# RWKV-7 units of a two-layer recurrent trunk: the centring of the values moved behind the second products, and one cast moved from VectorE to ScalarE

## The chip, the cores and the metric

The kernel runs on one core of one Trainium2 chip. The metric is device time in microseconds, from the start to the end of one execution. The kernel before took 2766.95 us (median of 3 runs, 2766.32 to 2776.49).

The engines are named as in the profile: PE is TensorE's matrix product and PEld its weight load, DVE is VectorE, ACT is ScalarE, POOL is GpSimd, SP is SyncE, which here only issues DMAs. ScalarE and GpSimd issue DMAs as well.

## The reference, cut to what matters

The model has two layers over 1024 positions of width 1024. Layer 0 is not touched by the change. Layer 1 is RWKV-7 time mixing with 32 heads of 64 channels:

```python
r, k_raw, v = x_r @ w_r, x_k @ w_k, x_v @ w_v
...
def step(state, inp):
    r_t, w_t, k_t, v_t, kk_t, a_t = inp
    s_kk = jnp.einsum("bhvk,bhk->bhv", state, kk_t)
    state = (state * w_t[:, :, None, :]
             - s_kk[..., None] * (kk_t * a_t)[:, :, None, :]
             + v_t[..., None] * k_t[:, :, None, :])
    y_t = jnp.einsum("bhvk,bhk->bhv", state, r_t)
    return state, y_t
...
mean = jnp.mean(y, axis=-1, keepdims=True)
y = ((y - mean) * lax.rsqrt(var + GN_EPS)).reshape(bsz, s, RW_WIDTH) * lnx_g + lnx_b
```

The kernel takes the scan in chunks of 64 positions. Inside a chunk the recurrence becomes a triangular system, whose inverse is worked out and then multiplied in. Because the output is centred over the 64 channels of a head anyway, the kernel centres the values `v` before the recurrence (a product with `cent`, the identity less 1/64).

## The kernel before, in words

Layer 1 is cut into 32 **units**: a quarter of the positions (256, `qt`) by a pair of 128-channel blocks (`pp`), so eight 64-by-64 chunks for each of the two heads in a block. Each unit goes through stages, written as generators that stop at every `yield`:

- `stage_g` (L935): the three projections `g<-x,w_kr`, `g<-x,w_r`, `g<-x,w_v`, 96 steps of six matmuls; their weights come by DMAs that SyncE issues.
- `stage_a` (L968): decays, normalised keys and the products `pa` of a chunk; its L1007 to L1014 (a clamp, Ln, Exp and products) stand around the change, and L987, L983 and L991 are early work of a later unit.
- `stage_i` (L1065): the inversion of the 32-by-32 triangles, step by step on VectorE (L1084, L1086), with a DMA round trip before (L1039, L1070) and after it (L1089, L1093).
- `stage_v` (L1097): `pvt`, the values centred and turned (8 matmuls), which ScalarE copies in four pieces into the two `uv` tiles (L1106); at its second step `pr`, a product with `uv`, copied to `ar` (L1114).
- `stage_l` (L1118): the two halves of the inverse joined (`pl`, behind VectorE's transpose L1124).
- `stage_s` (L1155): first the product of the inverse `xb` with `ar`, in two halves (`p1` in the code, `p<-ar,xb` in the profile). Each half is read from PSUM three times: `t1`, called T1 here (L1168, ScalarE), and the two halves of the partitions of `uv` (L1169 on VectorE, L1170 on ScalarE). Then `p2` (`p<-am,t` in the profile), which reads `t1` and `am`, again in two parts, read by VectorE as `gm` and `rp` (L1183, L1184); then `ph` and `py`, and the state's steps over four chunks (`sts`, `sper`, L1221).
- `stage_n` (L1229): the norm of the output.

**The order.** `program` (L1351) is a list written by hand, run once for each of the units `s`: `s0` takes the next step of `stage_s` for unit `s`, `i1`, `v1` and `l1` a step of those stages for unit `s + 1`, `a2` a step of `stage_a` for unit `s + 2`, and a number that many steps of `stage_g` for unit `s + 3`. TensorE's instructions all go through `mm` and `tr` (L881, L884), which pin them to exactly this order. The other engines' instructions are put in order by the framework's planner, with a timeline of its own; it may take work of a later unit forward where it sees an engine free.

**Shared space.** The PSUM tile of `p1`, `p2` and `pvr` is one bank with one buffer (`s` in L859 to L867): the second half of `p1` can only start when all three readers of the first half have ended, and `p2` only when all three of the second have. `pvt`, `pr0` and `pl` share another (`b`). `uv` has four buffers, two for each unit. In units 4 and 5 of each quarter (and near them) `stage_x` (L809) mixes the inputs of the next quarter, on ScalarE (L829, L832), VectorE (L830) and GpSimd (L833).

Of the kernel before, what the change touches and what calls it, by code (L numbers as in the profile page):

```python
# [31 lines left out]
def trunk_kernel(ctx: ExitStack, tc: tile.TileContext, I, out, dbg=None):  # L32
    nc = tc.nc
    V, S, G, PE = nc.vector, nc.scalar, nc.gpsimd, nc.tensor
# [566 lines left out]
    ur = (slice(64, 128), slice(0, 64))  # L601
# [195 lines left out]
    for p in range(NPAIR):  # L797
        for _ in range(-(-len(left) // (NPAIR - p))):
            j, q = left.pop(0)
# [49 lines left out]
    def W1(tag, bufs=1, shape=(P, TH), dtype=F32, name=None):  # L849
        return w1p.tile(list(shape), dtype, tag=tag, bufs=bufs, name=name or tag)  # L850
# [18 lines left out]
    def pu(use):  # L869
        return pp[0].tile([P, 512], F32, tag=pmap[use], bufs=pcnt[pmap[use]], name=use)  # L870
# [10 lines left out]
    def mm(*args, **kw):  # L881
        return pin(PE.matmul(*args, **kw))  # L882
# [177 lines left out]
    def cs(c):  # L1060
        return slice(c * 64, c * 64 + 64)
# [93 lines left out]
    def stage_s(u):  # L1155


        qt, pp_ = u["qt"], u["pp"]
        lc, pt, am, ar, uv = (u[n_] for n_ in ("lc", "pt", "am", "ar", "uv"))


        t1 = W1("t1", bufs=1, shape=(P, 8, 64))
        for q in range(2):
            p1 = pu("p1")
            for j in range(4):
                mm(p1[:, j * P:(j + 1) * P], xb[:, q * 4 + j, :], ar[:, :, q * 4 + j, :], start=True, stop=True)
            p1 = p1.rearrange("p (j s c) -> p j s c", s=2, c=64)
            S.copy(t1[:, q * 4:q * 4 + 4], p1[:, :, 0])  # L1168
            V.tensor_copy(uv[q][ur[0], 0], p1[ur[0], :, 1])  # L1169
            S.copy(uv[q][ur[1], 1], p1[ur[1], :, 1])  # L1170
            yield

        gm = W1("gm", bufs=1, shape=(P, NCH, 64))
        rp = W1("rp", bufs=1, shape=(P, NCH, 64))
        for e in range(2):
            p2 = pu("p2")
            for g in range(4):
                for h in range(2):
                    mm(p2[hr[h], g * P:(g + 1) * P], t1[ur[e], 2 * g + h, :],
                       am[g // 2][ur[e], h, 2 * (g % 2) + e, 64:192], start=True, stop=True,  # L1180
                       tile_position=(ur[e].start, hr[h].start))
            p2 = p2.rearrange("p (g s c) -> p g s c", s=2, c=64)
            V.tensor_tensor(gm[:, e::2], p2[:, :, 1], id2.unsqueeze(1).broadcast_to([P, 4, 64]), op=add)  # L1183
            V.tensor_tensor(rp[:, e::2], p2[:, :, 0], pt[:, 8 + e::2], op=add)  # L1184
            yield
            if e == 0:

                ph = pu("ph")
                for c in range(NCH):
                    for h in range(2):  # L1190
                        j = (c // 2) * 2 + h
                        mm(ph[hr[h], cs(c)], am[c // 4][:, h, c % 4, P:192], uv[c // 4][:, c % 2, j % 4, :],
                           start=(c == 0), stop=False, skip_group_check=True)
                py = pu("py")
                for c in range(NCH):
                    for h in range(2):
                        j = (c // 2) * 2 + h
                        mm(py[hr[h], cs(c)], uv[c // 4][:, c % 2, j % 4, :], am[c // 4][:, h, c % 4, 64:128],
                           start=(c == 0), stop=False, skip_group_check=True)
                yield  # L1200
        sts = W1("sts", bufs=1, shape=(P, 4, 2, 64))
        st = None if qt == 0 else sper[:, 2 * pp_:2 * pp_ + 2, :]
        ysb = W1("t1", bufs=1, name="ysb")
        for c in range(4):
            last = c == 3
            if st is not None and not (last and qt == 3):
                for i in range(2):
                    for h in range(2):
                        mm(ph[hr[h], cs(4 * i + c)], gm[hr[h], 4 * i + c, :], st[hr[h], i, :], start=False, stop=True,
                           tile_position=(hr[h].start, hr[h].start), skip_group_check=True)  # L1210
            if st is not None:
                for i in range(2):
                    for h in range(2):
                        mm(py[hr[h], cs(4 * i + c)], st[hr[h], i, :], rp[hr[h], 4 * i + c, :], start=False, stop=True,
                           tile_position=(hr[h].start, hr[h].start), skip_group_check=True)
            if last:
                S.copy(ysb, py)  # L1217
            if last and qt == 3:
                break
            nst = sper[:, 2 * pp_:2 * pp_ + 2, :] if last else sts[:, c]  # L1220
            V.tensor_tensor(nst, ph.rearrange("p (i c k) -> p i c k", i=2, k=64)[:, :, c],  # L1221
                            lc.rearrange("p (i c) -> p i c", i=2)[:, :, c:c + 1].broadcast_to([P, 2, 64]), op=mult)
            st = nst
            if not last:
                yield
        u["py"] = ysb
        yield
# [99 lines left out]
    def go(st_, i, k=1):  # L1327

        if 0 <= i < n:
            if (st_, i) not in gens:  # L1330
                gens[st_, i] = stages[st_](units[i])
            for _ in range(k):
                next(gens[st_, i], None)

    stages = dict(a=stage_a, i=stage_i, v=stage_v, l=stage_l, s=stage_s, n=stage_n)
    sixes = [0]
    gq, xq = [], []

    def fill(k=1):
# [9 lines left out]


    program = """  # L1351
        a2 s0 2 i1 v1 i1 s0 1 i1 a2 1 i1 s0 1 s0 1 i1 s0 1 v1 1 i1 s0 1 a2 1 i1 s0 1 i1 a2 1 i1 s0 1 i1 s0 n0 1
        a2 1 i1 a2 1 a2 i2 1 n0 l1 1 i2 a3 l1 3 i2 l1 i2 1 i2 1 a3 i2 1""".split()

    def prepare(k):
# [66 lines left out]
```

## Time and profile before

| | |
|---|---|
| runs, median (lowest to highest) | 2766.95 us (2766.32 to 2776.49) |
| the profiled execution's own time | 2771.17 us |
| its span, first to last instruction | 2769.4 us |
| mean granted TensorE clock | 0.972 of full speed |
| busy: PE, PEld, DVE, ACT, POOL | 92%, 80%, 62%, 44%, 24% of the span |
| HBM traffic | 203 GB/s over the span |

The profile is of one execution. Its page gives busy shares and the costliest groups of instructions. Behind it the trace can be asked for waits (which engine stood idle before which instruction, and what released it), for groups by line, for a timeline of one engine, and for busy time and granted clock in any stretch. A name such as `p<-am,t` is the tile written and the tiles read. Times in a timeline are us from the span's start. A product's end is modelled, so the products of TensorE overlap a little in the rows.

### The profile page before, as it was taken

To read this page: it belongs to the slowest core of one execution; us is meant where nothing else is said; L and a number is where in the kernel's file an instruction comes from. 1 tells how busy PE (TensorE), PEld (TensorE's weight loads), DVE (VectorE), ACT (ScalarE), POOL (GpSimd) and SP (SyncE) were. 2 spreads that over 40 slices of the span, in tenths; PEclk is the share of its full clock that TensorE was granted. 3 is DMA by queue.
4 is the path that set the end of the run, shared out by engine and by line. 5 is a ranking of instruction groups with operands and counts; after the bars stand their busy time and mean duration, and the time that the engine had idled before them with its cause. 6 is when DMAs were issued, how large, how long until landed. Compare 5 with 4: busy or idle time off the path is not lost.

```text
span 2769.4 us, 56914 instructions
## 1 busy us (share of the span) xinstructions
PE 2549.4 (92%) x22203; PEld 2214.3 (80%) x22203; DVE 1728.9 (62%) x4058; ACT 1226.1 (44%) x2439; POOL 654.7 (24%) x648
## 2 busy tenths in 40 slices
PE   7999999999999989997988999889998899998988
PEld 6777878788998766586887888778887788887988
DVE  5466566557657586245787676777767777677221
ACT  5466555555444455433345343453434434443221
POOL 2355444451116450111112011121111211110001
PEclk9999999999999999898999999999999999999999
DMA  6576666674564567685667576666765667666574
GB/s 202 170 254 223 217 212 224 222 255 141 190 192 137 178 198 223 207 293 177 191 210 225 183 221 191 201 203 210 227 198 189 208 204 221 202 211 186 170 266 151
DMA packets 531232, 566.50 MB, mean 205 GB/s; under 512 B 237745, under 2 KB 420242, under 8 KB 530962
## 3 DMA queue, kind: packets, MB, share of 16 engines
q1 hardware_dynamic: 473906, 481.50, 55.4%
q10 hardware_dynamic: 56192, 79.19, 8.7%
q8 instruction: 174, 2.85, 0.4%
q0 software_dynamic: 864, 2.18, 0.2%
q14 instruction: 96, 0.79, 0.1%
HBM read 428.52 MB, written 134.22 MB: 203 GB/s over the span
## 4 chain that ended last, share of the span: by engine, by line
PE 42%; DMA 17%; DVE 15%; issue 8%; ACT 6%; POOL 5%; SPq 4%; ACTq 0%; DVEq 0%; POOLq 0%
PE g L882 12%; PE pa L882 3%; DMA wd<-ht 3%; PE acc L882 3%; PE ph L882 3%; PE p L882 3%; POOL ht L382 2%; SPq L1093 2%; DVE xi L1086 2%; DVE itmp L1084 2%; PE py L882 2%; DMA y1d<-gt 2%; DMA x<-xd 2%; DMA nb<-nd 2%; SPq L1070 2%
## 5 line engine op out<-in xcount | busy, mean ns | idle before, releaser
L882 PE MATMUL g<-x,w_kr 128*128 128x256 f32 x1536 | 243.1, 301 | 8.2 <-DMA w_kr<-wd 8.2
L882 PE MATMUL g<-x,w_r 128*128 128x256 f32 x1536 | 247.1, 298 | 2.3 <-DMA w_r<-wd 2.3
L882 PE MATMUL g<-x,w_v 128*128 128x256 f32 x1536 | 232.7, 301 | 12.4 <-DMA w_v<-wd 12.3
L1086 DVE TENSOR_TENSOR xi<-xi,itmp 128x60 f32<-128x60 f32 (+21 forms) x864 | 222.5, 258 | 24.0
L382 POOL TENSOR_TENSOR ht<-ht 128x512 fp32r<-128x512 f32 x128 | 191.7, 1508 | 183.3 <-ACT ht L381 136.4
L1084 DVE TENSOR_TENSOR itmp<-xi,nb 128x60 f32<-128x60 f32 (+21 forms) x864 | 220.5, 255 | 22.5
L882 PEld LDWEIGHTS g<-x,w_kr 128*128 128x128 f32 x1536 | 206.6, 197 | 27.6 <-issue 19.5
L882 PEld LDWEIGHTS g<-x,w_v 128*128 128x128 f32 x1536 | 198.6, 194 | 32.7 <-DMA w_v<-wd 16.0
L882 PEld LDWEIGHTS g<-x,w_r 128*128 128x128 f32 x1536 | 199.6, 191 | 17.5 <-DMA w_r<-wd 2.5
L249 PE MATMUL acc<-wL_o,y 128*128 128x256 f32 x512 | 144.5, 286 | 7.1 <-DVE wL_o L183 7.1
L247 PE MATMUL acc<-wH_o,y 128*128 128x256 f32 x512 | 139.1, 285 | 4.2 <-ACT wH_o L182 2.0
L250 PE MATMUL acc<-wH_o,y 128*128 128x256 f32 x512 | 142.6, 283 | 0.0
L1074 POOL TENSOR_SCALAR xi<-eye 128x256 f32<-128x256 f32 x32 | 27.5, 861 | 469.0 <-DMA xd<-xi 388.6
L381 ACT CAST ht<-ht 128x512 fp32r<-128x512 f32 x128 | 78.2, 617 | 120.1 <-DMA wd<-ht 55.8
L882 PE MATMUL acc<-w_o,y 128*128 128x256 f32 x960 | 119.8, 288 | 7.3 <-DVE y L1263 4.2
L882 PEld LDWEIGHTS acc<-w_o,y 128*128 128x128 f32 x960 | 118.4, 196 | 8.6 <-DVE y L1263 4.9
L882 PE MATMUL p<-am,t 64*64 64x128 f32 x1024 | 73.6, 285 | 52.1 <-ACT uv L1170 52.1
L997 DVE TENSOR_TENSOR P<-r,lam 128x512 f32<-128x512 f32 x32 | 49.7, 1552 | 113.6 <-ACT r L953 113.6
L1036 DVE TENSOR_TENSOR am<-pa,rwm 128x512 f32<-128x512 f32 x128 | 85.4, 687 | 56.3 <-PE pa L882 56.1
L1217 ACT COPY ysb<-py 128x512 f32<-128x512 f32 x32 | 18.8, 587 | 229.2 <-PE py L882 229.2
L833 POOL TENSOR_TENSOR x<-xm,x 128x512 fp32r<-128x512 f32 x48 | 65.6, 1371 | 210.2 <-ACT x L832 210.2
L199 PE MATMUL gr<-g,wL_g 128*128 128x512 f32 x256 | 105.5, 412 | 9.4 <-DVE wL_g L183 9.3
(391 smaller groups left out, 6614.9 us busy)
## 6 DMA issues: line engine op xcount, KB each, us to landing
w_kr<-wd SPq DMA_DIRECT2D x128, 512.0 KB, 6.7
w_r<-wd SPq DMA_DIRECT2D x128, 512.0 KB, 4.1
w_v<-wd SPq DMA_DIRECT2D x128, 512.0 KB, 3.9
wd<-ht SPq DMA_DIRECT2D x96, 512.0 KB, 3.6
w_o<-wod SPq DMA_DIRECT2D x64, 512.0 KB, 3.4
wod<-ht SPq DMA_DIRECT2D x32, 512.0 KB, 3.6
wst_o<-in_ab_w_out_dram SPq DMA_DIRECT2D x64, 256.0 KB, 3.2
wst_g<-in_c_w_g_dram SPq DMA_DIRECT2D x64, 256.0 KB, 3.0
```

What stands on the lines that cost most here:

```text
L199: PE.matmul(ps, l[k], xh[k], start=False, stop=(k == NK - 1))
L247: PE.matmul(o, yH[kt][:, ts_], wh[j], start=(first and tb % 2 == 0), stop=False, skip_group_check=True)
L249: PE.matmul(o, yH[kt][:, ts_], wl[j], start=False, stop=False, skip_group_check=True)
L250: PE.matmul(o, yL[kt][:, ts_], wh[j], start=False, stop=last, skip_group_check=True)
L381: i = S.copy(hl[:, 0].bitcast(F32R), st)
L382: G.tensor_tensor(hl[:, 1].bitcast(F32R), st, hl[:, 0], op=sub)
L833: G.tensor_tensor(xl, x, xh.bitcast(F32), op=sub)
L882: return pin(PE.matmul(*args, **kw))
L1036: V.tensor_tensor(am[q][:, h, :, 0:P], pa.rearrange("p (c t) -> p c t", t=P), rwm.unsqueeze(1).broadcast_to([P, 4, P]), op=mult)
L1070: nc.sync.dma_start(nb[32 * g:32 * g + 32], u["nd"].rearrange("(p x) -> p x", x=2080)[:, 0:2048].rearrange("p (m s) -> p m s", s=64)[:, :, ...
L1084: V.tensor_tensor(t3, xi[:, 0:n, m:m + 1].broadcast_to([P, n, w]), nb[:, m:m + 1, m + 1:32].broadcast_to([P, n, w]), op=mult)
L1086: V.tensor_tensor(xi[:, 0:n, m + 1:32], xi[:, 0:n, m + 1:32], t3, op=add)
```

## The change

The step `v1` that makes `pvt` is taken out from between the two halves of `p1` and put behind the first part of `p2`. The cast of `uv` on L1169 is made by ScalarE in place of VectorE, so that the three readers of the bank are three ScalarE instructions in a row.

```diff
@@ -1166,8 +1166,8 @@
             p1 = p1.rearrange("p (j s c) -> p j s c", s=2, c=64)
             S.copy(t1[:, q * 4:q * 4 + 4], p1[:, :, 0])
-            V.tensor_copy(uv[q][ur[0], 0], p1[ur[0], :, 1])
-            S.copy(uv[q][ur[1], 1], p1[ur[1], :, 1])
+            for e in range(2):
+                S.copy(uv[q][ur[e], e], p1[ur[e], :, 1])
             yield
@@ -1349,7 +1349,7 @@
     program = """
-        a2 s0 2 i1 v1 i1 s0 1 i1 a2 1 i1 s0 1 s0 1 i1 s0 1 v1 1 i1 s0 1 a2 1 i1 s0 1 i1 a2 1 i1 s0 1 i1 s0 n0 1
+        a2 s0 2 i1 i1 s0 1 i1 a2 1 i1 s0 v1 1 s0 1 i1 s0 1 v1 1 i1 s0 1 a2 1 i1 s0 1 i1 a2 1 i1 s0 1 i1 s0 n0 1
         a2 1 i1 a2 1 a2 i2 1 n0 l1 1 i2 a3 l1 3 i2 l1 i2 1 i2 1 a3 i2 1""".split()
```

## Rows read from the trace of the kernel before

**Rows 1.** The page's first table: engine, busy us, share of the span, instructions.

```profile
PE 2549.4 (92%) x22203; PEld 2214.3 (80%) x22203; DVE 1728.9 (62%) x4058; ACT 1226.1 (44%) x2439; POOL 654.7 (24%) x648
```

**Rows 2.** What TensorE waited for, 1220 to 2600 us: total us, times, longest.

```profile
PE p L882 <- ACT uv L1170: 63.3, 42, 5.4
PE pl L882 <- DVE x L1124: 44.0, 52, 11.6
PE g L882 <- DMA w_v<-wd: 12.0, 15, 2.0
```

**Rows 3.** Groups by line: count, busy us, mean ns, idle time before and its releaser.

```profile
L882 PE MATMUL p<-am,t 64*64 64x128 f32 x1024 | 73.6, 285 | 52.1 <-ACT uv L1170 52.1
...
L1169 DVE COPY uv<-p 64x256 f32<-64x256 f32 x64 | 27.4, 427 | 17.3 <-ACT t L1168 15.3
...
L1170 ACT COPY uv<-p 64x256 f32<-64x256 f32 x64 | 23.3, 364 | 22.1 <-DVE uv L1169 21.8 <-DVE itmp L1084 0.3
```

**Rows 4.** A quiet unit, timeline of TensorE: start, us, instruction, idle before.

```profile
2383.04 1.05 PE L882 MATMUL pvt<-cent,v 128*128 128x128 f32 x8
2383.93 1.06 PE L882 MATMUL p<-ar,xb 128*128 128x128 f32 x8
...
2387.85 1.09 PE L882 MATMUL p<-am,t 64*64 64x128 f32 x16 [0.97 <-ACT uv L1170]
...
2394.63 1.15 PE L882 MATMUL pr<-uv,am 64*64 64x64 f32 x32
```

**Rows 5.** The same unit, timeline of ScalarE.

```profile
2382.18 0.35 ACT L1168 COPY t<-p 128x256 f32<-128x256 f32 x1
2382.44 0.63 ACT L1009 ACTIVATE sqa<-sqa 128x512 f32<-128x512 f32 x1
2383.03 0.37 ACT L1170 COPY uv<-p 64x256 f32<-64x256 f32 x1
...
2384.13 1.50 ACT L1106 COPY uv<-pvt 64x256 f32<-64x256 f32 x4 [0.73 <-PE pvt L882]
2385.66 0.37 ACT L1168 COPY t<-p 128x256 f32<-128x256 f32 x1
2385.93 0.64 ACT L987 ACTIVATE lam<-cum 128x512 f32<-128x512 f32 x1
2386.46 1.08 ACT L983 ACTIVATE k<-a,kam,prm 128x256 f32<-128x256 f32 x2
...
2387.70 0.63 ACT L991 ACTIVATE cum<-cum 128x512 f32<-128x512 f32 x1
...
2395.83 0.59 ACT L1114 COPY ar<-pr 128x512 f32<-128x512 f32 x1 [7.50 <-PE pr L882]
```

**Rows 6.** The same unit, timeline of VectorE.

```profile
2382.57 0.43 DVE L1169 COPY uv<-p 64x256 f32<-64x256 f32 x1
...
2386.97 0.43 DVE L1169 COPY uv<-p 64x256 f32<-64x256 f32 x1
...
2399.33 0.69 DVE L1036 TENSOR_TENSOR am<-pa,rwm 128x512 f32<-128x512 f32 x1 [0.50 <-PE pa L882]
```

**Rows 7.** A turn unit, timelines of TensorE, ScalarE and VectorE, 1776 to 1800 us.

```profile
1787.21 1.97 PE L882 MATMUL p<-am,t 64*64 64x128 f32 x16 [5.43 <-ACT uv L1170]
...
1782.26 0.37 ACT L1168 COPY t<-p 128x256 f32<-128x256 f32 x1
...
1786.33 0.43 DVE L1169 COPY uv<-p 64x256 f32<-64x256 f32 x1
...
1789.22 0.42 DVE L1183 TENSOR_TENSOR gm<-p,id 128x256 f32<-128x256 f32 x1 [0.62 <-PE p L882]
...
1795.82 0.43 DVE L1183 TENSOR_TENSOR gm<-p,id 128x256 f32<-128x256 f32 x1 [1.97 <-PE p L882]
```

**Rows 8.** The same unit, stretch behind the wait: busy us (x), then granted clock.

```profile
1787.20:1794.00 6.80, 6.79 (x87) 6.17 (x88) 5.48 (x23) 0.76 (x2) 0.00 (x0) 0.56 0.31 77
```

## The prediction

> **What bounds the kernel now.** I read the page's first table first: TensorE is busy 92% of the span and VectorE 62% [rows 1]. Busy time is an average, so the next view is what TensorE waits for, in the stretch from 1220 to 2600 us in which all the instructions of the diff lie [rows 2]. In those 1380 us TensorE, whose order is fixed by hand, stands still before three things: 63.3 us before products into `p` until the copy of L1170 has ended, 44.0 us before `pl` until VectorE's transpose of L1124, 12.0 us for a weight tile. The change aims at the first. The groups by line [rows 3] show that 52.1 of the 63.3 us lie before the second products (`p<-am,t`, called P2 below); the remaining 11.2 lie before the second half of the first products (`p<-ar,xb`, P1). They also show why: of the three readers that empty the one PSUM bank of `p`, the middle one is on VectorE, and ScalarE's last copy stood idle 21.8 us for it.
>
> The timelines show two kinds of unit. **A quiet unit** [rows 4, 5]: P1's second half starts at 2383.93, right behind `pvt`; its product is read by ScalarE only from 2385.66, after four copies of `pvt` (1.50 us); VectorE's copy ends at 2387.40 [rows 6]; ScalarE's last copy follows, and P2 starts at 2387.85 after 0.97 us of nothing [rows 4]. **A turn unit**, in which the next quarter's inputs are mixed on VectorE [rows 7]: VectorE gets to its copy only at 1786.33, 3.7 us after the copy of T1 ended (1782.63), and TensorE stands 5.43 us. There are five of these (5.41, 5.43, 4.51, 5.13 and 3.05 us; one is shown), 23.5 us together. The other 27 units share 52.1 - 23.5 = 28.6 us, 1.06 us each.
>
> **The change, part by part.** All times of the working are in the profiled execution, 2771.17 us with a span of 2769.4; the median of the runs is 2766.95, 4.2 us less, and I take the same difference off the median.
>
> *VectorE's copy goes to ScalarE.* 64 copies of 0.427 us, 27.4 us, leave VectorE [rows 3]; 64 of 0.37 us, 23.4 us, are added to ScalarE. The bank is then emptied by three ScalarE instructions in a row, with no wait on another engine: four such copies of `pvt` take 1.50 us [rows 5], so three take about 1.12. As the rows stand, the first half is emptied from 2382.18 to 2383.40, with Exp (L1009, 0.63 us) between the first and the last copy. That Exp is written ahead of the copies and is ready when T1 is out, so I let it keep its place: T1 2382.18, Exp to 3.07, two copies from 2383.03 to 2383.78. The bank is then free 0.4 us later than now. The other end is Exp behind the copies, free at about 2383.30, 0.1 us earlier.
>
> On the pair of half copies a rule speaks against the change. Rows first: VectorE's copy runs from 2382.57 to 2383.00 and ScalarE's starts at 2383.03; the 21.8 us of idle time show the same order elsewhere [rows 3, 5, 6]. The Trainium skill, PSUM — Partial Sum Buffer, section "PSUM bank collisions raise a hardware error", says that two engines may use one bank at once when they are in different quarters of the partitions, as these halves are; by that the halves could run side by side, the row would cost about 0.3 us more per half unit than a pair run together, and the sum would lose up to 64 x 0.3 = 19 us. In this trace they do not run side by side, so I take nothing off.
>
> *The centring moves behind P2.* `pvt` is 8 matmuls, 0.89 us to the next start (2383.04 to 2383.93), and four ScalarE copies, 1.50 us; its step issues no DMA, so on SP and POOL nothing changes place, and on ScalarE's queue the copies pass only the issue of one gate load and the work of the next unit (L987, L983, L991). Where it stands now, `pvt` costs TensorE nothing but hides 0.89 us of emptying P1's first half. Without it TensorE arrives at P1's second half at 2383.04 and, with Exp kept, stands until 2383.83: a new wait of 0.79 us (0.29 with Exp behind). The four copies no longer stand before the second reading of T1. P1's second half then starts at 2383.83, ends at 2384.89, its three copies follow at once and end at 2386.05; TensorE arrives at P2 2.9 us after that start (now 2386.88 after 2383.93 [rows 4]), about 2386.7, and finds no wait, also if L987 (0.6 us) comes first. P2 starts 1.15 us earlier than now, then `pvt` takes its 0.89: 0.26 us saved (0.76 with Exp behind). Where P1 is already late, the saving is nearer to 0. I take 0.3 us for each of 27 units, 8 us, between 0 and 19.
>
> Behind P2 the copies of `pvt` are needed by `pr` (6.8 us after P2 in this unit, 2394.63 against 2387.85 [rows 4]), and ScalarE is idle 7.50 us before it reads `pr` [rows 5]. So 1.50 us there costs nothing; if that cover were gone it would cost 32 x 1.5 = 48 us, which the 7.50 excludes.
>
> *Turn units.* T1's second half stays where it is, 1782.26, since other ScalarE work precedes it; two copies behind it end near 1783.4, and P2 could start then, against 1787.21 now. It comes 3.8 us earlier, less 0.89 for `pvt`: 2.9 us. What is late next is VectorE itself, which must give `gm`. It is idle for TensorE there 0.62 and 1.97 us [rows 7], and gets 0.86 us back from two copies: 3.4 us bound the gain of such a unit, so 2.9 stands in most; with 2.0 for the 3.05 us unit, 13 us for five. After the long wait the granted clock is 0.56 over 6.8 us [rows 8], that is mostly the 1.2 GHz level, and 0.44 x 6.8 = 3.0 us of matmul time; I count none of it, since VectorE caps these units, and up to 5 us in the upper end.
>
> *What gives back.* In a quiet unit VectorE is without idle time from before P1 until it waits 0.50 us for `pa` [rows 6]. It can follow a TensorE that is up to 0.50 + 0.86 = 1.4 us faster, which 0.3 to 0.8 does not exceed. The waits for weights (12.0 us) and for `pl` (44.0 us) hang on transfers and may grow; I take off 3 us, between 0 and 15.
>
> Sum: 8 + 13 - 3 = 18 us saved: 2771 to 2753 in the profiled execution, 2749 by the median.
>
> **The rivals.** *Exp behind the copies.* The planner orders ScalarE by its own timeline; if the copies go first, quiet units give 0.6 us, 16 us, turn units the same 13 and some clock: 32 us, 2735. For it: T1 already stands ahead of Exp [rows 5].
>
> *The gain is taken back elsewhere.* The inversion's chain (transpose, two DMAs, `pl`) may set the pace; TensorE already waits for it 44.0 us, with 52 waits [rows 2]. If all but the turn units' VectorE time is taken back, 5 us are left: 2762. Against: VectorE's 0.50 us of idle time and the 27 us that leave it.
>
> *Slower: T1's second reading goes behind hoisted work.* With the four `pvt` copies gone, ScalarE has a hole in front of it, in which the planner can put L987, L983 and L991 (0.64 + 1.08 + 0.63 us), which now follow T1 and the copies [rows 5]. From about 2384.9 on they take to 2387.0; three copies later P2 starts at 2388.2, 0.3 us later than now, and `pvt` still follows: 1.2 us per quiet unit, 27 x 1.2 = 32, less 13: 19 us slower, 2786. It decides from T1 starting 0.9 us after P1's second half has ended (2385.8). Against: L983 and L991 stand behind L987 in the rows, and L987 comes up late. In the Trainium skill, the same page, section "Engine vs sequencer instructions", ScalarE's queue is strictly first in, first out, so T1 could not pass them; the order in the rows agrees.
>
> **How the numbers follow.** Forecast (about 11 to 24 us saved) 0.45, Exp behind 0.2, taken back 0.26, slower 0.09. About 0.5%, 13.8 us, is what a measurement of this kernel can tell from no change, so faster means under 2753. Exp behind lies there wholly and three quarters of the forecast: 0.2 + 0.34 = 0.54. Slower by over 0.5% is the last rival, 0.09. The rest, 0.37, is within. The low end takes quiet units at 19, turn units at 13 and 5 for the clock, nothing given back: 37 us, with a little beyond it, 2727. The high end takes in the gain wholly taken back, and a small loss: 2769. Left out are the slower rival and a tenth at the fast end.
>
> **What would show it.** Right: no VectorE row of L1169 or `uv<-p`; the wait before P2 falls from 52.1 us to under 15, that before P1 rises from 11.2 to 25 to 45; `pvt` stands behind P2; the five long waits are gone, `gm` no longer waits for TensorE. Wrong: a wait before P2 of over 30 us (T1 behind hoisted work), waits before `pl` or weights that grow by over 15 us, or P1's wait above 50.

## The result and the profile after

The changed kernel took 2749.32 us (median of 4 runs, 2743.63 to 2752.64), against 2771.72 us for the kernel before in the same rounds: ratio 0.9901, 95% interval 0.9876 to 0.9926 (the quotient of the two medians, 0.9919, lies inside). In a second job the ratio was 0.9924 (0.9904 to 0.9945). The forecast was 2749 us, and its range 2727 to 2769 holds the time. The kernel before has a fourth run here (2778.24 us), which lifts its median by 4.8 us over the one that the forecast started from. By the medians 22.4 us were saved where 18 were forecast, and that the two times agree to a microsecond is chance. The span of the profiled execution fell from 2769.4 to 2748.9 us, its mean granted clock from 0.972 to 0.968. In the last two experiments below one of six executions took over twice as long (5823 and 6463 us, mean granted clock 0.43 and 0.51); their ratios are of the other five, and the cause was not looked for.

First the page's table of busy times of the changed kernel; it answers to [rows 1].

```profile
PE 2557.4 (93%) x22203; PEld 2222.8 (81%) x22203; DVE 1693.9 (62%) x3994; ACT 1256.4 (46%) x2503; POOL 659.0 (24%) x648
```

VectorE has 64 instructions and 35 us fewer, ScalarE 64 and 30 us more: the cast has moved. The waits of TensorE from 1220 to 2600 us show where the time came from; they answer to [rows 2].

```profile
PE pl L882 <- DVE x L1124: 47.3, 48, 11.7
PE p L882 <- ACT uv L1170: 29.0, 23, 4.5
PE g L882 <- DMA w_v<-wd: 10.1, 13, 1.6
PE pa L882 <- DVE am L1036: 8.5, 6, 2.4
```

The kernel before had this row for the last of them:

```profile
PE pa L882 <- DVE am L1036: 2.8, 3, 1.5
```

The wait for the bank of `p` fell from 63.3 to 29.0 us. Of these 34.3 us, 3.3 came back before `pl` and 5.7 before `pa`, and the span is 20.5 us shorter. TensorE's busy time is 8.0 us longer for the same number of instructions; a second trace of the changed kernel has 2548.6 us, less than before the change, so this part is not the change's. The groups by line, which answer to [rows 3], show that the wait did not shrink evenly but changed its place.

```profile
L882 PE MATMUL p<-ar,xb 128*128 128x128 f32 x512 | 73.4, 288 | 30.2 <-ACT uv L1170 28.8
L882 PE MATMUL p<-am,t 64*64 64x128 f32 x1024 | 70.0, 276 | 0.2 <-ACT uv L1170 0.2
```

Before P2 0.2 of 52.1 us are left. Before P1 there are 30.2 us, against this row of the kernel before:

```profile
L882 PE MATMUL p<-ar,xb 128*128 128x128 f32 x512 | 70.9, 282 | 11.4 <-ACT uv L1170 11.2
```

The same quiet unit as in [rows 4, 5], now on the timeline of TensorE and then on that of ScalarE:

```profile
2359.04 1.67 PE L882 MATMUL g<-x,w_kr 128*128 128x256 f32 x12
2360.86 1.16 PE L882 MATMUL p<-ar,xb 128*128 128x128 f32 x8
...
2363.84 1.09 PE L882 MATMUL p<-am,t 64*64 64x128 f32 x16
2364.86 1.16 PE L882 MATMUL pvt<-cent,v 128*128 128x128 f32 x8
```

```profile
2359.69 0.35 ACT L1168 COPY t<-p 128x256 f32<-128x256 f32 x1
2360.06 0.75 ACT L1170 COPY uv<-p 64x256 f32<-64x256 f32 x2
2360.71 0.63 ACT L1009 ACTIVATE sqa<-sqa 128x512 f32<-128x512 f32 x1
...
2362.47 0.38 ACT L1168 COPY t<-p 128x256 f32<-128x256 f32 x1 [1.14 <-PE p L882]
2362.86 0.75 ACT L1170 COPY uv<-p 64x256 f32<-64x256 f32 x2
2363.51 0.63 ACT L987 ACTIVATE lam<-cum 128x512 f32<-128x512 f32 x1
...
2366.12 1.50 ACT L1106 COPY uv<-pvt 64x256 f32<-64x256 f32 x4 [0.34 <-PE pvt L882]
```

Three copies in a row empty the bank in 1.12 us (2359.69 to 2360.81), as worked out. But the planner put them ahead of Exp (L1009), not behind it, so the bank is free before TensorE has gone far: P1's second half starts 0.05 us after the copies. T1's second reading starts as soon as its product is there (ScalarE waited 1.14 us for it), the moved copies of `pvt` stand behind everything, and P2 follows without a wait.

A turn unit, the same as in [rows 7]:

```profile
1767.20 0.37 ACT L1168 COPY t<-p 128x256 f32<-128x256 f32 x1 [0.21 <-PE p L882]
1767.59 0.75 ACT L1170 COPY uv<-p 64x256 f32<-64x256 f32 x2
...
1768.98 1.09 PE L882 MATMUL p<-am,t 64*64 64x128 f32 x16
```

The 5.43 us are gone. The remaining wait is of another kind; here is its longest case, in unit 1 (units are counted from 0), on the timelines of TensorE, ScalarE and VectorE. `pn` is the product of `stage_a` that the clamp reads.

```profile
1301.25 1.02 PE L882 MATMUL pn<-sqa,bd 128*128 128x512 f32 x2
1302.10 1.05 PE L882 MATMUL p<-ar,xb 128*128 128x128 f32 x8
...
1309.05 2.08 PE L882 MATMUL p<-ar,xb 128*128 128x128 f32 x8 [4.46 <-ACT uv L1170]
...
1307.35 0.63 ACT L1008 ACTIVATE sqa<-sqa 128x512 f32<-128x512 f32 x1 [2.60 <-DVE sqa L1007]
...
1307.88 0.35 ACT L1168 COPY t<-p 128x256 f32<-128x256 f32 x1
...
1306.63 0.68 DVE L1007 TENSOR_SCALAR sqa<-pn 128x512 f32<-128x512 f32 x1
```

P1's first half (from 1302.10, 1.05 us long) was done at 1303.15, but T1 was read only at 1307.88: on ScalarE's queue it stands behind Ln (L1008), which waits for VectorE's clamp (L1007). `pn`, which the clamp reads, was done at 1302.27, but VectorE came to the clamp only at 1306.63, 4.4 us later and without a pause before it, behind steps of the inversion. The bank's emptying still hangs on VectorE's queue, one instruction further up. Where the clamp follows `pn` at once, as in the quiet unit, P1 waits only 0.15 us.

### The profile page after: what moved, and what is told of

Its sections match the earlier page's. It is cut to its first block, busy times and chain, and to the rows that moved or that the text cites. A ratio compares the mean times of both kernels' runs of the same rounds, so it can differ in the third digit from the quotient of the medians.

```text
span 2748.9 us, 57007 instructions
## 1 busy us (share of the span) xinstructions
PE 2557.4 (93%) x22203; PEld 2222.8 (81%) x22203; DVE 1693.9 (62%) x3994; ACT 1256.4 (46%) x2503; POOL 659.0 (24%) x648
## 4 chain that ended last, share of the span: by engine, by line
PE 46%; DMA 15%; DVE 14%; issue 9%; ACT 6%; POOL 6%; SPq 4%; ACTq 0%; DVEq 0%; POOLq 0%
PE g L882 13%; PE pa L882 4%; DMA wd<-ht 3%; PE p L882 3%; PE acc L882 3%; POOL ht L382 2%; DVE itmp L1084 2%; PE ph L882 2%; DMA w_v<-wd 2%; SPq L1070 2%; DVE xi L1086 2%; DMA nb<-nd 2%; PE py L882 2%; SPq L1093 2%; PE gr L199 1%
## 5 line engine op out<-in xcount | busy, mean ns | idle before, releaser
L1084 DVE TENSOR_TENSOR itmp<-xi,nb 128x60 f32<-128x60 f32 (+21 forms) x864 | 232.4, 269 | 22.8
L882 PE MATMUL g<-x,w_v 128*128 128x256 f32 x1536 | 235.0, 303 | 10.4 <-DMA w_v<-wd 10.3
L1086 DVE TENSOR_TENSOR xi<-xi,itmp 128x60 f32<-128x60 f32 (+21 forms) x864 | 204.0, 236 | 23.5
L882 PE MATMUL pa<-P,BK 64*128 64x128 f32 x1024 | 115.3, 294 | 8.5 <-DVE am L1036 8.5
L882 PEld LDWEIGHTS pa<-P,BK 64*128 64x128 f32 x1024 | 102.6, 195 | 17.5 <-DVE am L1036 9.8
```

Of the source, the lines that this page charges most:

```text
L1084: V.tensor_tensor(t3, xi[:, 0:n, m:m + 1].broadcast_to([P, n, w]), nb[:, m:m + 1, m + 1:32].broadcast_to([P, n, w]), op=mult)
L1086: V.tensor_tensor(xi[:, 0:n, m + 1:32], xi[:, 0:n, m + 1:32], t3, op=add)
```

## The experiments

All ratios are to the kernel before, in the same job, with 95% intervals. The last table of this section puts the waits beside the times.

### The cast alone

The program of before, with the three readers on ScalarE:

```diff
-            V.tensor_copy(uv[q][ur[0], 0], p1[ur[0], :, 1])
-            S.copy(uv[q][ur[1], 1], p1[ur[1], :, 1])
+            for e in range(2):
+                S.copy(uv[q][ur[e], e], p1[ur[e], :, 1])
```

> Only the cast of L1169 goes to ScalarE; the centring stays between the two halves of P1. Theory A (the gain is VectorE's lateness taken out of the emptying of the bank; the move of the centring only shifts a wait from P2 to P1): the wait before P2 falls from 52 us to under 12, that before P1 from 11 to under 10, the five long waits are gone; time at or below that of the full change: ratio to the kernel before 0.985 to 0.991. Theory B (the centring must move too, since its four copies, 1.50 us, stand before the second reading of T1): the wait before P2 stays over 20 us and the ratio is 0.993 to 0.998.

Measured: 2744.27 us, ratio 0.9857 (0.9818 to 0.9896). Theory A held, but for P2's wait, 14.6 us where under 12 was expected.

```profile
L882 PE MATMUL p<-ar,xb 128*128 128x128 f32 x512 | 71.7, 285 | 9.4 <-ACT uv L1170 9.3
L882 PE MATMUL p<-am,t 64*64 64x128 f32 x1024 | 69.8, 275 | 14.6 <-ACT uv L1170 12.7 <-DVE itmp L1084 1.7
```

Both waits are short: 9.4 us before P1, where `pvt` still covers the emptying, and 14.6 before P2. The cast alone removes more waiting than the whole change (24.0 against 30.4 us left).

### The move alone

The program of the change, with VectorE's cast kept:

```diff
-        a2 s0 2 i1 v1 i1 s0 1 i1 a2 1 i1 s0 1 s0 1 i1 ...
+        a2 s0 2 i1 i1 s0 1 i1 a2 1 i1 s0 v1 1 s0 1 i1 ...
```

> Only the centring moves behind P2; VectorE keeps its cast. Theory A: VectorE is still the middle reader of three, so the long waits before P2 stay (3 to 5 us in the turn units), the wait before P1 grows from 11 us to over 25, and the ratio to the kernel before is 0.997 to 1.004. Theory B: without the four copies ahead of T1 most of P2's wait goes, ratio 0.990 to 0.995.

Measured: 2786.41 us beside 2783.55, ratio 1.002 (0.9997 to 1.0043). Theory A held again by its ratio and by P1's wait; its long waits before P2 stayed in one turn unit only.

```profile
L882 PE MATMUL p<-ar,xb 128*128 128x128 f32 x512 | 74.7, 291 | 43.1 <-ACT uv L1170 43.1
L882 PE MATMUL p<-am,t 64*64 64x128 f32 x1024 | 71.1, 279 | 24.9 <-ACT uv L1170 24.9
```

The move halves P2's wait and nearly quadruples P1's; the sum is 68.0 us, 4.5 more than before. In the five units of the long waits 23.5 us before P2 became 7.3, and 3.6 before P1 became 14.3: VectorE's lateness is still there, but mostly one product earlier. This is the unit that kept the longest wait before P2 (3.93 us, beside 5.43 in the kernel before):

```profile
1775.95 1.47 PE L882 MATMUL p<-ar,xb 128*128 128x128 f32 x8 [2.42 <-ACT uv L1170]
1784.47 1.97 PE L882 MATMUL p<-am,t 64*64 64x128 f32 x16 [3.93 <-ACT uv L1170]
```

### The full change with Exp kept ahead

The order that the prediction had assumed, given to the planner as an order without a wait:

```diff
-        S.activation(sq, sq, AF.Exp, scale=-0.5)
+        lexp[0] = S.activation(sq, sq, AF.Exp, scale=-0.5)
...
-                S.copy(uv[q][ur[e], e], p1[ur[e], :, 1])
+                i = S.copy(uv[q][ur[e], e], p1[ur[e], :, 1]); q or lexp[0] is None or after(i, lexp[0])
```

> The full change, with an order given to the planner: the two uv copies of P1's first half come behind Exp (L1009), as the prediction had assumed. If waits of TensorE before P1 count in full: the bank is free 0.5 to 0.6 us later in the 27 units, the wait before P1 grows from 30 us to 42 to 48, and the time by 8 to 14 us over that of the full change (ratio to the kernel before 0.993 to 0.997). If VectorE sets the pace instead (it waits 25 times for this Exp, 7.5 us in all, in the changed kernel): the wait before P1 grows as much, but the time stays within 4 us of the full change (0.989 to 0.992).

Measured: 2781.30 us, ratio 0.9989 (0.9969 to 1.001). Nearly the whole gain is gone, more than either theory said. The last row is the page's table of busy times.

```profile
L882 PE MATMUL p<-ar,xb 128*128 128x128 f32 x512 | 78.3, 301 | 59.8 <-ACT uv L1170 58.8 <-ACT xb L1152 0.9
L882 PE MATMUL p<-am,t 64*64 64x128 f32 x1024 | 69.9, 276 | 0.0
...
L1008 ACT ACTIVATE sqa<-sqa 128x512 f32<-128x512 f32 x32 | 20.2, 631 | 57.2 <-DVE sqa L1007 57.2
...
PE 2563.6 (92%) x22203; PEld 2227.2 (80%) x22203; DVE 1700.6 (61%) x3994; ACT 1251.1 (45%) x2503; POOL 657.6 (24%) x648
```

The wait before P1 doubled, from 30.2 to 59.8 us. Exp's place, 0.5 us in some 30 units, would be 15 us of that. The rest goes with Ln: it waited 57.2 us for VectorE's clamp, against 45.5 in the changed kernel, so T1 came later too. The planner had also given VectorE another order, so this run is not Exp's place alone. Waits before P1 count for the larger part: some 30 us more of them went with 0.65 to 0.88% (18 to 24 us) more time. The run shows one thing more. VectorE has lost the 64 copies here as in the changed kernel (28.3 us less busy than before), but the waits before P1 and P2 are about as long as before (59.8 us, beside 63.5), and so is the time. Here VectorE's lighter load alone, without a shorter wait, gained nothing that can be told from zero.

### P1's first half ahead of `pn`

The full change, with `s0` first in the program, so that T1's first reading is not behind Ln:

```diff
-        a2 s0 2 i1 i1 s0 1 i1 a2 1 i1 s0 v1 1 s0 1 i1 ...
+        s0 a2 2 i1 i1 s0 1 i1 a2 1 i1 s0 v1 1 s0 1 i1 ...
```

> The full change, and the first half of P1 stands ahead of the step of stage_a that makes pn. The reading of T1 then no longer stands behind Ln (L1008), which waits for VectorE, and the bank is emptied behind pn and twelve products. If TensorE's wait before P1 sets the pace: it falls from 30 us to under 6 and the time by 15 to 25 us below the full change (ratio to the kernel before 0.980 to 0.985). If the chain of pn, Ln, Exp, kk and pa does, which starts 0.9 us later in each unit: waits before pa grow from 8.5 us to over 20 and the ratio stays 0.988 to 0.993.

Measured: 2736.02 us, ratio 0.9829 (0.9796 to 0.9861), as the first theory had it, with 7.2 us before P1 where under 6 was expected.

```profile
L882 PE MATMUL p<-ar,xb 128*128 128x128 f32 x512 | 71.8, 285 | 7.2 <-ACT uv L1170 5.3 <-ACT xb L1152 1.9
L882 PE MATMUL p<-am,t 64*64 64x128 f32 x1024 | 70.1, 276 | 8.4 <-ACT uv L1170 7.8 <-DVE itmp L1084 0.5
```

P1's wait falls from 30.2 to 7.2 us, and P2's rises from 0.2 to 8.4. Waits before `pa` fell from 8.5 to 6.1 us, so the later `pn` cost nothing there; those before `pl` and for `w_v` rose by 5.0 and 4.3 us. The wait that the changed kernel had left goes when Ln no longer stands ahead of T1.

### The full change and the cast alone, again, in the same rounds

> The full change once more, on the same chip and in the same rounds as the next three. By the first runs: ratio to the kernel before 0.988 to 0.992.

> The cast alone once more, beside the full change. If the move of the centring costs time where the cast is on ScalarE (TensorE's waits before P1 and P2 are 22 us in this kernel against 29 us in the full change): ratio 0.984 to 0.988, 3 to 10 us below the full change. If the move is neutral: within 3 us of the full change.

Measured: the full change 2759.75 us, 0.9924 (0.9904 to 0.9945); the cast alone 2740.81 us, 0.9864 (0.9837 to 0.9891). The intervals do not meet: once the cast is on ScalarE, the move costs 0.6% (0.0060 of 2783 us, 17 us), more than expected. The waits for `p` are 36.2 us (36.0 and 0.2) against 23.8 (9.5 and 14.3), 12 us apart; the spans of the two executions that these waits are read from lie 8.8 us apart (2756.9 and 2748.1), so the waits cover the difference there. Why the medians lie further apart than these two executions is not shown.

### The cast alone, with P1's first half ahead of `pn`

The program of before with `s0 a2` in place of `a2 s0`, and the cast on ScalarE.

> The cast alone, with the centring where it was, and the first half of P1 ahead of the step that makes pn. If emptying is then hidden behind pn, twelve products and the centring: the wait before P1 is under 4 us, that before P2 10 to 20 us (four copies of pvt in front of T1's second reading), ratio 0.980 to 0.984, as with the full change and P1 first (0.983). If the copies in front of T1 decide: P2's wait is over 25 us and the ratio 0.986 to 0.990.

Measured: 2744.61 us, ratio 0.9879 (0.9854 to 0.9904), the second case, at least by its time. P1's wait fell to 5.5 us, but P2's rose to 22.3 (expected: under 4, and 10 to 20): T1's second reading stands behind the four copies of `pvt`. Unit 10, on the timelines of ScalarE and TensorE:

```profile
1687.49 1.50 ACT L1106 COPY uv<-pvt 64x256 f32<-64x256 f32 x4 [0.23 <-issue]
1689.01 0.37 ACT L1168 COPY t<-p 128x256 f32<-128x256 f32 x1
...
1690.19 1.09 PE L882 MATMUL p<-am,t 64*64 64x128 f32 x16 [1.18 <-ACT uv L1170]
```

So the place of the copies does matter. That the products may stay where they are is shown by the last two experiments.

### Work given back to VectorE

The full change, with 64 additions on VectorE that nobody reads:

```diff
+            V.tensor_tensor(dum, id2.unsqueeze(1).broadcast_to([P, 6, 64]), id2.unsqueeze(1).broadcast_to([P, 6, 64]), op=add); yield
```

> The full change, and VectorE gets 64 additions of 128x384 elements that nobody reads, about as long as the 64 copies that left it (0.43 us each), so it is as busy as before but nobody waits for it. If only the wait on VectorE counted: ratio as in the full change, within 3 us. If the 27 us of work taken from VectorE counted, as the prediction's bound for the turn units has it: 8 to 20 us slower than the full change, ratio 0.993 to 0.997.

Measured: 2768.40 us, ratio 0.9953 (0.9937 to 0.9968), 8.7 us above the full change in these rounds. By its time this is the second case, but the run does not test it: the additions wait for nothing in a unit, and the planner put all 64 of them ahead of the units. A row gives the shortest, the median and the longest duration in ns, then the first and the last start in us.

```profile
L1171 DVE TENSOR_TENSOR dum<-id x64: 544/557/1528, 1171.6 to 1233.0; 128x384 f32<-128x384 f32 x64
L882 PE MATMUL p<-ar,xb x512: 272/275/422, 1269.5 to 2586.0; 128*128 128x128 f32 x171
```

The last addition starts at 1233.0 us, the first P1 at 1269.5. In the repeat of the full change the first P1 starts at 1262.0, 7.5 us earlier, and from there to the first P1 of the last unit the two kernels take the same, 1313.3 us with the additions and 1314.6 without. The 8.7 us are lost ahead of the units, so this run says nothing of what VectorE's lighter load is worth inside them.

### Products of `g` between the halves of P1

The full change, with one step of six products taken from behind P1's second half to ahead of it:

```diff
-        a2 s0 2 i1 i1 s0 1 i1 a2 1 i1 s0 v1 1 s0 1 i1 ...
+        a2 s0 3 i1 i1 s0 i1 a2 1 i1 s0 v1 1 s0 1 i1 ...
```

> The full change with six products of g moved from behind P1's second half to ahead of it (three steps of stage_g between the halves, none right behind). If the short wait before P1 is lost cover, as the prediction has it: the wait before P1 falls from 30 to 35 us to 10 to 18, P2 (emptying 1.2 us, cover down to 1.2 us) gets 3 to 10 us, and the ratio goes from 0.990-0.992 to 0.984 to 0.989. If the time hangs on the inversion's chain: ratio stays at 0.990 or above while the wait before P1 falls.

Measured: 2726.28 us, ratio 0.9824 (0.9796 to 0.9851). The waits are 6.6 us before P1 and 6.9 before P2. 0.9 us of other products as cover do for P1 what `pvt` had done (9.4 us in the cast alone), and the gain is a little more than expected. The inversion's chain did not take it back.

### `pvt` as cover, its copies out of the way

The cast alone; the eight products stay between the halves of P1, and their four copies are ordered behind the last copy of P1's second half:

```diff
             mm(pvt[:, g * P:(g + 1) * P], vT[:, g * P:(g + 1) * P], cent, start=True, stop=True)
+        yield
...
-                S.copy(uv[q][hr[e], e], pvt[...])
+                i = S.copy(uv[q][hr[e], e], pvt[...]); luv[0] is None or after(i, luv[0])
...
-                S.copy(uv[q][ur[e], e], p1[ur[e], :, 1])
+                luv[0] = S.copy(uv[q][ur[e], e], p1[ur[e], :, 1])
...
-        a2 s0 2 i1 v1 i1 s0 1 i1 a2 1 i1 s0 1 s0 1 i1 ...
+        a2 s0 2 i1 v1 i1 s0 v1 1 i1 a2 1 i1 s0 1 s0 1 i1 ...
```

> The cast alone, the eight products pvt stay between the halves of P1 as cover, and only their four ScalarE copies come behind the emptying of P1's second half. If the two places of ScalarE's queue are what counts: the waits before P1 and P2 together fall from 22 us (cast alone) to under 12, that before P2 under 2, ratio 0.980 to 0.985. If pvt's copies then come too late for pr: a wait before pr of over 5 us and no gain over the cast alone (0.986).

Measured: 2722.95 us, ratio 0.9812 (0.9777 to 0.9848).

```profile
L882 PE MATMUL p<-ar,xb 128*128 128x128 f32 x512 | 70.1, 281 | 8.7 <-ACT uv L1171 8.6
L882 PE MATMUL p<-am,t 64*64 64x128 f32 x1024 | 69.8, 275 | 2.6 <-DVE rp L1185 2.0 <-ACT uv L1171 0.6
...
L882 PE MATMUL pr<-uv,am 64*64 64x64 f32 x1024 | 36.7, 221 | 0.0
```

P2's wait falls from 14.6 to 2.6 us (expected: under 2), and `pr` waits for nothing.

### Both: the copies behind, and P1's first half ahead of `pn`

As above, with `s0 a2` in place of `a2 s0`.

> As the run before, and the first half of P1 stands ahead of the step that makes pn. Waits before P1 and P2 together under 4 us, ratio 0.977 to 0.982, faster than every other version. If the waits for pl and the weights take it back: p under 4 us, but pl and weights together over 75 us and the ratio not under 0.983.

Measured: 2711.83 us, ratio 0.9767 (0.9736 to 0.9798), the fastest version: 1.4% below the changed kernel by their ratios. A quiet unit of it, on the timelines of TensorE and ScalarE (lines from L1107 on are one further down):

```profile
2327.56 1.05 PE L882 MATMUL pvt<-cent,v 128*128 128x128 f32 x8
2328.45 1.06 PE L882 MATMUL p<-ar,xb 128*128 128x128 f32 x8
...
2331.32 1.09 PE L882 MATMUL p<-am,t 64*64 64x128 f32 x16
...
2325.48 0.37 ACT L1169 COPY t<-p 128x256 f32<-128x256 f32 x1 [0.31 <-PE p L882]
2325.86 0.74 ACT L1171 COPY uv<-p 64x256 f32<-64x256 f32 x2
2327.19 0.63 ACT L1008 ACTIVATE sqa<-sqa 128x512 f32<-128x512 f32 x1 [0.59 <-DVE sqa L1007]
...
2329.54 0.37 ACT L1169 COPY t<-p 128x256 f32<-128x256 f32 x1 [1.06 <-PE p L882]
2329.93 0.75 ACT L1171 COPY uv<-p 64x256 f32<-64x256 f32 x2
2330.58 1.50 ACT L1107 COPY uv<-pvt 64x256 f32<-64x256 f32 x4
```

In this unit each reading of the bank starts when its product is there, and both products of `p` start without a wait. Over all units 9.7 us are left before P1 and P2, where under 4 were expected. Waits before `pl` (49.7 us) and for `w_v` (8.5) did not grow against the changed kernel by more than 2.4 us, so nothing took the gain back.

The waits of TensorE before the two products, in us and each read from one execution, beside the ratios:

| kernel | before P1 | before P2 | ratio |
|---|---|---|---|
| before | 11.4 | 52.1 | 1 |
| move alone | 43.1 | 24.9 | 1.002 |
| full change, Exp ahead | 59.8 | 0.0 | 0.9989 |
| full change, additions on VectorE ahead of the units | 29.8 | 1.4 | 0.9953 |
| full change | 30.2, again 36.0 | 0.2, again 0.2 | 0.9901, again 0.9924 |
| cast alone, P1 first | 5.5 | 22.3 | 0.9879 |
| cast alone | 9.4, again 9.5 | 14.6, again 14.3 | 0.9857, again 0.9864 |
| full change, P1 first | 7.2 | 8.4 | 0.9829 |
| full change, `g` between | 6.6 | 6.9 | 0.9824 |
| cast, copies behind | 8.7 | 2.6 | 0.9812 |
| cast, copies behind, P1 first | 7.4 | 2.3 | 0.9767 |

The kernels stand in the order of the sum of the two columns, but for two: the first two rows, whose times cannot be told apart, and the one with the additions, which loses its time elsewhere. From the first row to the last the sum falls by 53.8 us and the time by 61 us (2773.08 to 2711.83, in one job).

## Why the prediction was right

**The total was right; one step of the working was wrong, and a second error, no smaller, stood against it.** The steps:

*VectorE's copy to ScalarE: right.* Three copies in 1.12 us, one behind the other, no wait on VectorE between them. The cast alone shows that this is the whole gain (0.9857, again 0.9864), with the move 0.9901 and 0.9924. Nothing came of the penalty worked out from the rule of the Trainium skill on two engines in different partition quarters of a bank (PSUM — Partial Sum Buffer, "PSUM bank collisions raise a hardware error"): up to 19 us were put beside it, and the cast alone is faster by 42 us in its second job (2741 against 2783). No run here shows two engines reading the bank at once, so the rule itself was not tried.

*"So I let it keep its place": wrong.* This is the step that failed. The planner put the copies ahead of Exp, as the first rival had it. In the run that kept Exp ahead, in which VectorE's order was another too, the change saves 0.1%, not the 18 us of the forecast.

*The quiet units: the term was too large for the order that came about.* With Exp behind, the working gave 0.76 us a unit, 16 us by the rival. From the first P1 of unit 0 to that of unit 31, without the three blocks of the next paragraph, the kernel before took 781.6 us, the changed one 775.0 and in its repeat 783.3: 6.7 us less and 1.6 us more, each from one execution. The wait before P1 is 30.2 us in 32 units, 0.94 us each, not 0.29: T1 often stands behind Ln, which waits for VectorE. The prediction saw units "where P1 is already late" and gave them "nearer to 0", but not that this is what would be left. P1 ahead of `pn` shows it: the wait falls to 7.2 us and the ratio to 0.9829. The better order was worth 8 us more by the working, and the late T1 took 9 us off that in one trace and 18 in the other; that the sum still met the time is luck in this part.

*The centring behind P2: the price was right, the sign of the whole was not asked.* "`pvt` costs TensorE nothing but hides 0.89 us" was the key sentence, and the signs given for right (P1's wait 25 to 45 us, P2's under 15) came out as 30.2 and 0.2. But the two parts were only summed together. Alone, the move gains nothing (1.002), and beside the cast it costs 0.6%. What it was good for, the four copies out of T1's way, can be had without giving up the cover.

*The turn units: right in size, not in place.* The blocks of four units with the turns, from the start of P1 in units 4, 12 and 20 to that in units 8, 16 and 24, took 185.2, 180.5 and 177.5 us before and 177.2, 177.8 and 175.5 after: 12.7 us less, 12.0 less in the repeat, forecast 13. The forecast put 2.9 us into most of the five units of the long waits, and these did not get shorter, 241.2 us before and 242.7 after. Counted from P1's start, P2 starts some 30 us earlier in the five together, and then TensorE waits for VectorE: before `pl` 17.8 us (5.4 before), before `pa` 7.9 (0.4). The gain lies in the other seven units of the blocks, where the wait before `pl` falls from 10.4 to 2.0 us. The cap itself was right: in the five units VectorE waited 5.6 us for TensorE before `gm`, and now waits for nothing there (over all units it is 17.8 us before and 25.4 after, but 5.7 and 18.4 of these are in the last unit). What VectorE's 27 us less of work are worth in these units no run shows apart.

*What gives back: right in kind.* 3 us were taken off; over all units `pl` and `pa` took 9.0 us more, `w_v` and `w_kr` (3.3 to 2.4 us) 2.8 less.

*The slower rival* did not come: T1's second reading starts on time and L987 stands behind it.

## What to carry to other kernels

Where several engines read one PSUM bank in turn, look at which of them has the longest queue; the bank is free when that one gets to it, and a row of copies on the engine with room removes its lateness. Work of TensorE that stands between a product and its reuse of a bank is cover, and here it cost nothing; before moving it away, move only its readers out of the queue that empties the bank. Price the parts of a change alone as well as together, and where a planner orders a queue, carry both orders to the end of the sum: here keeping Exp ahead, with what the planner changed beside it, left 0.1% of a gain of 1%. Before reading an experiment by its time, look in its trace whether the edit did its work where it was meant to: the additions on VectorE did not.

## What the runs showed of the hardware that was not expected

Where the long waits before P2 went, the 2.4 GHz level came back, but the mean of the span did not rise. In the 6.8 us from P2's start the granted clock was 0.57 to 0.75 in the five units before and is 1.00 in all five now; this is the unit of [rows 8] (busy us of each engine, then granted clock, DMA share and GB/s).

```profile
1768.90:1775.70 6.80, 6.80 (x118) 6.08 (x116) 6.61 (x18) 5.07 (x12) 2.92 (x4) 1.00 0.58 182
```

The 1.2 GHz level now shows behind other waits: in unit 1, behind the 4.46 us before P1, the granted clock is 0.51 from 1309.0 to 1311.2 us, and P1 took 2.08 us for eight products, against 1.16 in the quiet unit; behind 7.08 us before `pl` it is 0.60 from 2187.6 to 2194.4. The mean of the span, 0.972 before and 0.968 after, is 0.975 in the repeat of the same changed kernel, so it shows nothing of the change. An addition of 128x384 fp32 elements on VectorE, with both inputs read as a repeated 64-column tile, took 557 ns in the median, where 0.43 us had been expected.
